# Weights of a later stage split into two parts ahead of time and kept in DRAM

## Chip, cores and metric

The kernel runs on one NeuronCore of one Trainium2 chip. The metric is device time in microseconds (us), the median of several executions.

## Reference

The computation is ten stages over one activation of 512 tokens by 1024 features, in fp32. The first block has two layers, each a mixer and a feed-forward; the second block has two layers of its own, each a mixer, a cross-attention to 256 memory tokens and a feed-forward. What matters here is the first block:

```
for l in range(2):                                   # first_block
    h = rmsnorm(x, norm_mix_g[l]);  proj = h @ w_in[l]          # "mixer": 1024 -> 4896 columns
    qa, ka, va, qd, kd, vd, beta, decay, z, gates = split(proj)
    y_attn = grid_attention(rope(rms(qa)), rope(rms(ka)), va) @ w_o_attn[l]
    o = bidir_gated_deltanet(conv(qd), conv(kd), conv(vd), sigmoid(beta), decay)
    y_dn = (rmsnorm(o) * silu(z)) @ w_o_dn[l]
    x = x + (sigmoid(g0) * y_attn + sigmoid(g1) * y_dn) @ w_out[l]
    h = rmsnorm(x, norm_ffn_g[l]);  u_gate, u_val = conv3(h @ w_up[l])   # "feed-forward"
    x = x + (silu(u_gate) * u_val) @ w_down[l]
```

## The kernel before

Activations lie transposed: eight tiles of 128 features by 512 tokens. The stages run in the order m0, f0, m1, f1 (first block), ev, xa0, g0, od, xa1, g1 (second block); `body` calls them one after the other. The framework builds each engine's instruction order from the order of the program and a simulated timeline, so instructions of later code can stand ahead of earlier code on an engine.

Every product of weights and activations is made of three TensorE passes: each fp32 value is split into a high part (rounded to the fast matmul format) and a low part (what is left), and `proj` (L487 to L495) adds high x high, high x low and low x high. Activations are split once. A weight group is 1024 rows by 256 columns (1 MiB). `fetch` (L463) loads it by one transfer on SP's queue (L465) into one of two buffers `wraw`. `wload` (L469) then cuts it into four pieces of 128 x 512 (two column halves, two row halves); for each, ScalarE casts the high part `whi` (L478) and GpSimd subtracts for the low part `wlo` (issued through the helper at L384). `whi` and `wlo` have four buffers each, that is one group. TensorE uses a piece for 12 matmuls, and a group for 48.

A mixer (`_mix`) uses 19 such groups of `w_in`: four for keys and queries of the delta rule (`qk_pair`), two for its values (`vproj`), two for z (`zproj`), one for attention's k and v (`qkv`), two for its queries (`queries`), and eight for the gates (`gate_logits`). Only the first four run alone. The others are generators that a class `Side` advances beside the long chains: `inside` (the chunks of the delta rule, which stores many small blocks to DRAM: `dn`, `scrN`, `scrT`), `solve` (a triangular solve on DVE, which begins with the loads of `N` from `scrN` and `scrT`, L1023 and L1024), `core` (attention) and `scan` (the states of the delta rule). After the scan come the branch products (`w_o_attn`, `w_o_dn`) and `w_out`.

A feed-forward (`ffn`) makes its 22 pairs of tiles in 11 steps `up_pair` (two groups each), and multiplies by `w_down` in three parts `down` through `out_proj` (four groups each): after 5, 9 and 11 pairs. The weights are laid out in DRAM by the host (`_pack_cols`) so that a group is one contiguous run of 8 KB in each partition; a piece is then four runs of 128 elements.

Of the kernel before, what the change touches and what calls it, by code (L numbers as in the profile page):

```python
# [44 lines left out]
def _pack_cols(w, kc, cg):  # L45

    w = np.asarray(w)
    L, K, N = w.shape
    g = N // cg
    a = w.reshape(L, kc, P, g, cg).transpose(0, 3, 2, 1, 4)  # L50
    return np.ascontiguousarray(a).reshape(L, g, P, kc * cg)


def _cols(v):
# [151 lines left out]
def host_arrays(inputs):  # L206
    g = lambda k: np.asarray(inputs[k])
    A = {}
    A["x"] = np.ascontiguousarray(g("x")[0].T).reshape(8, P, S)
    A["mem"] = _pack_cols(np.asarray(g("mem_2")).transpose(0, 2, 1), 8, NMEM)[0, 0]  # L210
    A["vec"] = _vec_layout(inputs)[1]
    A["cst"] = CST_ARR
    A["rope"] = np.ascontiguousarray(_rope_tables())
    A["rett"] = _ret_tables()
    A["hgm"] = _hg_masks()
    A["dsat"] = _dsa_tables()
    A["relb"] = np.concatenate([g("rel_bias_2"), np.ones((1, 8), np.float32)], axis=0)
    w = g("w_in")
    qa, ka, va = w[..., :512], w[..., 512:640], w[..., 640:768]
    qd, kd, vd = w[..., 768:1280], w[..., 1280:1792], w[..., 1792:2304]  # L220
    bd, z, gate = w[..., 2304:2336], w[..., 2336:2848], w[..., 2848:]

    by_head = lambda a: a.reshape(2, -1, 2, 2, 2, 64).transpose(0, 1, 2, 4, 3, 5).reshape(2, -1, 512)
    z = by_head(z)
    qa = qa.reshape(2, D, 4, P)[..., PERM_A].reshape(2, D, 512)
    ka = ka[..., PERM_A]
    A["win"] = _pack_cols(np.concatenate([kd, qd, vd, qa, ka, va, z, gate], axis=-1), 8, 256)
    A["wbd"] = _pack_cols(bd, 8, 32)
    A["woa"] = _pack_cols(g("w_o_attn"), 4, 128)
    A["wod"] = _pack_cols(by_head(g("w_o_dn").transpose(0, 2, 1)).transpose(0, 2, 1), 4, 128)  # L230
    A["wout"] = _pack_cols(g("w_out"), 8, 256)
    A["wup"] = _pack_cols(g("w_up"), 8, 256)
    for nm, key in (("wdn", "w_down"), ("fdn", "ffn_w_out_2")):
        w = g(key)
        A[nm] = np.concatenate([_pack_cols(w[:, :1024], 8, 256), _pack_cols(w[:, 1024:2048], 8, 256)], axis=1)
        A[nm + "c"] = _pack_cols(w[:, 2048:], 6, 256)
# [3 lines left out]
    A["evin"] = _pack_cols(np.concatenate(ev, axis=2).reshape(1, D, 4096), 8, 256)  # L240
    A["evout"] = _pack_cols(np.concatenate([eo[:, 1 - i, h] for i, h in EV_HEADS], axis=1), 8, 256)

    od = g("od_w_in_2").reshape(1, D, 3, 8, P).transpose(0, 1, 3, 2, 4).reshape(1, D, 3072)
    A["odin"] = _pack_cols(od, 8, 256)
    A["odout"] = _pack_cols(g("od_w_out_2"), 8, 256)
    A["xaq"] = _pack_cols(g("xa_w_q_2"), 8, 256)
    A["xakv"] = _pack_cols(g("xa_w_kv_2"), 8, 256)
    A["xao"] = _pack_cols(g("xa_w_o_2"), 8, 256)
    A["fup"] = _pack_cols(g("ffn_w_in_2"), 8, 256)
    return A  # L250


# [53 lines left out]
class Prog:  # L306
    def __init__(self, ctx, tc, A, out, first):
        self.ctx, self.tc, self.nc, self.A, self.out = ctx, tc, tc.nc, A, out
        nc = self.nc
        pool = lambda name, bufs=1, **kw: ctx.enter_context(tc.tile_pool(name=name, bufs=bufs, **kw))  # L310
        self.cp = pool("cp")
        self.xp = pool("xp")
        self.wr = pool("wr", 2)
        self.whl = pool("whl", 4)
        self.actp = pool("actp", 8)
        self.nrm = pool("nrm")
        self.psb_ = pool("psb", 2, space=PSUM)
        self.dr = pool("dr", 1, space=DRAM)
        self.ph = None
        self.mem = {}  # L320
# [139 lines left out]
        return ps  # L460


    def fetch(self, src, kc, cg):  # L463
        raw = self.wr.tile([P, kc, cg], F32, name="wraw", tag="wraw")
        self.nc.sync.dma_start(out=raw, in_=src.rearrange("p (k c) -> p k c", k=kc))  # L465
        return raw

    def wload(self, src, kc, cg, rows=False):


        nc = self.nc
        raw = self.first.pop(0) if self.first else self.fetch(src, kc, cg)
        step, width = (2, cg) if rows else (4, min(P, cg))

        def piece(k, o):
            part = raw[:, k:min(k + step, kc), o:o + width]
            hi, lo = (self.whl.tile(list(part.shape), F32R, name=n, tag=n) for n in ("whi", "wlo"))
            nc.scalar.copy(hi, part)  # L478
            self.tt(lo, part, hi.bitcast(F32), ALU.subtract, "gpsimd")
            return k, hi, lo  # L480

        return [[piece(k, o) for k in range(0, kc, step)] for o in range(0, cg, width)]

    def proj(self, ps, w, acts, n=S, behind=None):

# [48 lines left out]
    def out_proj(self, wsrc, acts, nxt, k0=0, scale=None, final=True, behind=None):  # L534
        nc = self.nc
        kc = len(acts)
        for g in range(4):
            ws = self.wload(wsrc[g][:, k0 * 256:(k0 + kc) * 256], kc, 256)
            for j in range(2):
                m = 2 * g + j  # L540
                ps = self.psb()
                self.proj(ps, ws[j], acts, behind=behind)
                if scale is None:
                    self.tt(self.x[m], ps, self.x[m], ALU.add)
                else:
                    nc.vector.scalar_tensor_tensor(self.x[m], ps, scale, self.x[m], ALU.mult, ALU.add)
                if final:
                    self.x_done(m, nxt)

    def x_done(self, m, nxt):  # L550
        nc = self.nc
# [10 lines left out]
    def ffn(self, l, second, nm, nxt):  # L562
# [3 lines left out]
        with self.phase("ffn") as fp, self.banks(2, 2):  # L566
# [48 lines left out]
            def up_pair(mp):  # L615
                wg = self.wload(wup[mp], 8, 256)
                wv = self.wload(wup[11 + mp], 8, 256)
                for j in range(2):
                    v = (up2 if second else up1)(2 * mp + j, wg[j], wv[j])
                    mid = self.gs("mid", 12, (P, 2, S), F32R)  # L620
                    self.split(mid, v)
                    mids[2 * mp + j] = mid

            def down(gi):
                ks = range(8 * gi, min(22, 8 * gi + 8))
                src = [wdn[gi * 4 + i] for i in range(4)] if gi < 2 else [wdnc[i] for i in range(4)]
                self.out_proj(src, [mids[k] for k in ks], nxt, final=gi == 2)

            for mp in range(5):
                up_pair(mp)  # L630
                if mp == 2 and l == 0 and second:
# [6 lines left out]
            down(1)  # L638
            for mp in range(9, 11):
                up_pair(mp)  # L640
            down(2)


# [4 lines left out]
    def _mix(self, l, nm, nxt, mp):  # L648
        nc, tc = self.nc, self.tc
        win = self.A["win"][l]  # L650
        col = lambda name, n=64: mp.tile([P, n], F32, name=name)
        blk64 = self.c("blk64")

# [52 lines left out]
        kq = []  # L706

        def qk_pair(g, first, a):
            ws = self.wload(win[g], 8, 256)
            for j in range(2):  # L710
                if a == 0:
                    kq.append(kv("kq", (first + j) // 2))
# [95 lines left out]

        def vproj():
            for g in range(4, 6):  # L810
                ws = self.wload(win[g], 8, 256)
                for j in range(2):
                    p = 2 * (g - 4) + j
                    c = th("cv", 2)
# [79 lines left out]
        def qkv():  # L894


            ws = self.wload(win[8], 8, 256)
# [18 lines left out]
        def queries(g):  # L916


            ws = self.wload(win[6 + g], 8, 256)
            qs = []  # L920
            for w in ws:
                qs.append(gained(w, f"qg{l}"))
# [66 lines left out]

        def zproj():  # L990
            for g in range(9, 11):
                ws = self.wload(win[g], 8, 256)
                for j in range(2):
                    if j == 0:
                        zz = kv("z", 0)
# [6 lines left out]

        def gate_logits(base, res, make):
            for g in range(4):
                ws = self.wload(win[base + g], 8, 256)
# [650 lines left out]
    def _cross(self, l, nm, nxt, xp):  # L1656
# [30 lines left out]
        for h in range(4):  # L1687
# [14 lines left out]
            ws = self.wload(wkv[4 + h], 8, 256, rows=True)  # L1702
            vt = [gs("vt", 4, (P, 2, M), F32R) for _ in range(2)]
            pv = [self.psb() for _ in range(2)]
            for t in range(2):
                tok = slice(t * P, (t + 1) * P)
                o = pv[t][:, :M]
                for k, hi, lo in ws[0]:
# [96 lines left out]
```

## Time and profile before

| | |
|---|---|
| median of 3 runs | 3369.54 us (3366.3 to 3373.71) |
| profiled execution: its time | 3364.51 us |
| its span, first to last instruction | 3362.7 us |
| mean granted TensorE clock | 0.986 of full |
| PE / DVE / ACT / POOL busy | 95% / 55% / 45% / 51% |
| f0 in the trace | about 480 to 885 us |
| m1 in the trace | about 885 to 1345 us |

PE is TensorE's matmuls, DVE is VectorE, ACT is ScalarE, POOL is GpSimd, SP is the engine whose queue issues nearly all transfers. Busy time of PE is modelled from its starts, so a PE that shows as fully busy is one that is never left waiting, not one at its peak. In a view of stretches, the number after a busy time is the count of instructions, PEclk is the granted clock as a share of full speed, and the DMA share is the mean busy share of the 16 DMA engines.

### The profile page before, as it was taken

Reading aid. Unit: us, or ns where it says so; the run is one execution under the profiler, and the core shown is the slowest. Engines: PE = TensorE matmul, PEld = TensorE weight load, DVE = VectorE, ACT = ScalarE, POOL = GpSimd, SP = SyncE. Lnnn points to the kernel's source line nnn. Section 1 sums busy time; section 2 is a strip of 40 time slices with the busy share of each in tenths; the row PEclk is TensorE's granted clock in tenths of the full one; section 3 lists DMA queues with packets and bytes.
Section 4 is the critical chain, followed back from the end, with each engine's and each line's share of the span. In section 5 each row is a group of like instructions: output and inputs, shape, how many; then the busy total and the mean of one; then the engine's idle time right before and its main releaser. Section 6 shows DMA issues by size and latency. Waiting matters only on the chain. (4 is left out here: it accounts for less than half of the span.)

```text
span 3362.7 us, 47054 instructions
## 1 busy us (share of the span) xinstructions
PE 3198.5 (95%) x17342; PEld 2643.8 (79%) x17342; DVE 1832.8 (55%) x3549; ACT 1499.9 (45%) x2804; POOL 1719.1 (51%) x1453
## 2 busy tenths in 40 slices
PE   8988799999998889999999998999999999999999
PEld 6767678888776677788887777878888888888887
DVE  7687556463678855555366675453223676453222
ACT  5646444343564643443353335543334455544332
POOL 4542375444554236544456556565556336555554
PEclk9999999999999999999999999999999999999999
DMA  4632532222355254322222113234223223222222
GB/s 155 179 94 67 136 118 99 97 92 94 125 162 136 69 124 129 126 90 99 100 102 88 63 47 129 91 124 132 90 99 110 73 69 126 95 91 93 99 100 88
DMA packets 142013, 353.03 MB, mean 105 GB/s; under 512 B 44079, under 2 KB 81327, under 8 KB 113112
## 3 DMA queue, kind: packets, MB, share of 16 engines
q1 hardware_dynamic: 140352, 346.53, 32.0%
q10 hardware_dynamic: 1432, 3.49, 0.4%
q8 instruction: 138, 2.26, 0.3%
q14 instruction: 91, 0.75, 0.1%
HBM read 316.34 MB, written 34.16 MB: 104 GB/s over the span
## 5 line engine op out<-in xcount | busy, mean ns | idle before, releaser
L384 POOL TENSOR_TENSOR wlo<-wraw,whi 128x512 fp32r<-128x512 f32 (+2 forms) x1044 | 1353.1, 1299 | 1420.8 <-ACT whi L478 1382.6
L478 ACT CAST whi<-wraw 128x512 fp32r<-128x512 f32 (+2 forms) x1044 | 633.4, 608 | 1141.0 <-PE psb L494 863.7
L491 PE MATMUL psb<-act,whi 128*128 128x512 f32 x1888 | 750.8, 398 | 25.4 <-ACT whi L478 12.6
L495 PE MATMUL psb<-act,wlo 128*128 128x512 f32 x1888 | 746.3, 396 | 0.6 <-POOL wlo L384 0.4
L494 PE MATMUL psb<-act,whi 128*128 128x512 f32 x1888 | 746.3, 395 | 0.6 <-DVE act L277 0.6
L491 PEld LDWEIGHTS psb<-act,whi 128*128 128x128 f32 x1888 | 359.0, 190 | 101.9 <-ACT whi L478 14.1
L495 PEld LDWEIGHTS psb<-act,wlo 128*128 128x128 f32 x1888 | 358.0, 190 | 76.5 <-POOL wlo L384 3.0
L494 PEld LDWEIGHTS psb<-act,whi 128*128 128x128 f32 x1888 | 358.6, 190 | 73.7 <-DVE act L277 2.0
L384 DVE TENSOR_TENSOR x<-psb,x 128x512 f32<-128x512 f32 x168 | 115.1, 689 | 380.3 <-PE psb L495 380.0
L491 PE MATMUL ps<-act,whi 128*128 128x512 f32 (+1 forms) x720 | 282.8, 393 | 3.4 <-ACT rB L303 3.4
L494 PE MATMUL ps<-act,whi 128*128 128x512 f32 (+1 forms) x720 | 282.2, 392 | 0.0
L495 PE MATMUL ps<-act,wlo 128*128 128x512 f32 (+1 forms) x720 | 281.9, 391 | 0.0
L491 PE MATMUL psb<-mid,whi 128*128 128x512 f32 x704 | 277.1, 394 | 1.0 <-DVE x L384 1.0
L495 PE MATMUL psb<-mid,wlo 128*128 128x512 f32 x704 | 276.3, 393 | 0.0
L494 PE MATMUL psb<-mid,whi 128*128 128x512 f32 x704 | 273.9, 389 | 0.0
L491 PEld LDWEIGHTS ps<-act,whi 128*128 128x128 f32 (+1 forms) x720 | 135.0, 188 | 34.3 <-ACT rB L303 4.9
L495 PEld LDWEIGHTS ps<-act,wlo 128*128 128x128 f32 (+1 forms) x720 | 135.0, 188 | 29.7
L494 PEld LDWEIGHTS ps<-act,whi 128*128 128x128 f32 (+1 forms) x720 | 135.0, 187 | 29.3
L495 PEld LDWEIGHTS psb<-mid,wlo 128*128 128x128 f32 x704 | 132.3, 188 | 30.5
L491 PEld LDWEIGHTS psb<-mid,whi 128*128 128x128 f32 x704 | 132.7, 188 | 29.2 <-DVE x L384 1.5
L494 PEld LDWEIGHTS psb<-mid,whi 128*128 128x128 f32 x704 | 132.2, 188 | 29.2
L384 DVE TENSOR_TENSOR cv<-ps,cv 128x512 f32<-128x512 f32 (+1 forms) x60 | 41.5, 692 | 188.7 <-PE ps L495 106.8
(431 smaller groups left out, 5441.9 us busy)
## 6 DMA issues: line engine op xcount, KB each, us to landing
wraw<-in_wup SPq DMA_DIRECT2D x44, 1024.0 KB, 4.8
wraw<-in_fup SPq DMA_DIRECT2D x44, 1024.0 KB, 4.8
wraw<-in_win SPq DMA_DIRECT2D x38, 1024.0 KB, 4.8
wraw<-in_wdn SPq DMA_DIRECT2D x16, 1024.0 KB, 4.8
wraw<-in_evin SPq DMA_DIRECT2D x16, 1024.0 KB, 4.8
wraw<-in_xakv SPq DMA_DIRECT2D x16, 1024.0 KB, 4.9
wraw<-in_fdn SPq DMA_DIRECT2D x16, 1024.0 KB, 4.9
wraw<-in_odin SPq DMA_DIRECT2D x12, 1024.0 KB, 4.8
```

Source lines behind the costliest of these rows:

```text
L384: getattr(self.nc, eng).tensor_tensor(out, a, b, op)
L478: nc.scalar.copy(hi, part)
L491: mm = nc.tensor.matmul(ps, hi[:, i], acts[k][:, 0, :n], start=k == 0, stop=False)
L494: nc.tensor.matmul(ps, hi[:, i], acts[k][:, 1, :n], start=False, stop=False)
L495: nc.tensor.matmul(ps, lo[:, i], acts[k][:, 0, :n], start=False, stop=k == kc - 1)
```

## The change

During f0, a generator `split_ahead` loads the 19 groups of `w_in` of layer 1, splits them and stores both parts to DRAM. It is advanced once after each `up_pair` and once after each group of the first two `down` parts (5 + 4 + 4 + 4 + 2 = 19 steps). A step loads two halves of 128 x 1024 (512 KB each), casts both on ACT, subtracts the first on DVE and the second on GpSimd, and issues the two stores (1 MiB each) of the step before. In m1, `wload_split` takes the place of `wload` for the 19 groups: eight transfers of 256 KB on SP's queue, straight into the four `whi` and four `wlo` buffers, with no cast and no subtraction. Also, the host lays out nearly all weights so that a piece is one contiguous run of 512 elements (`_pack_tiles`); the split of all other groups goes on as before, on such pieces. The stages m0 and all those from f1 on do the same work as before.

```diff
+def _pack_tiles(w, kc):
+    a = _pack_cols(w, kc, 256)
+    L, g = a.shape[:2]
+    return np.ascontiguousarray(a.reshape(L, g, P, kc, 2, P).transpose(0, 1, 2, 4, 3, 5)).reshape(L, g, P, kc * 256)
...
-    A["win"] = _pack_cols(np.concatenate([kd, qd, vd, qa, ka, va, z, gate], axis=-1), 8, 256)
+    A["win"] = _pack_tiles(np.concatenate([kd, qd, vd, qa, ka, va, z, gate], axis=-1), 8)
...
+    def fetch(self, src, kc, cg, k0=0, n=None):
+        n, w = n or kc, min(P, cg)
+        raw = self.wr.tile([P, cg // w, n, w], F32, name="wraw", tag="wraw")
+        self.nc.sync.dma_start(out=raw, in_=src.rearrange("p (j k c) -> p j k c", k=kc, c=w)[:, :, k0:k0 + n])
+        return raw
+    def parts(self, part):
+        nc = self.nc
+        hi, lo = (self.whl.tile(list(part.shape), F32R, name=n, tag=n) for n in ("whi", "wlo"))
+        nc.scalar.copy(hi, part)
+        self.tt(lo, part, hi.bitcast(F32), ALU.subtract, "gpsimd")
+        return hi, lo
+    def split_ahead(self, pool, name, groups):
+        nc = self.nc
+        late = []
+        for i, src in enumerate(groups):
+            dst = self.dr.tile([P, 2, 2, 1024], F32, name=f"{name}{i}")
+            self.ahead[name, i] = dst
+            for a in late:
+                nc.sync.dma_start(out=a[0], in_=a[1])
+            late = []
+            for j in range(2):
+                raw = pool.tile([P, 1024], F32, name="araw", tag="araw", bufs=2)
+                nc.sync.dma_start(out=raw, in_=src[:, j * 1024:j * 1024 + 1024])
+                t = pool.tile([P, 2, 1024], F32R, name="ahl", tag="ahl", bufs=4)
+                nc.scalar.copy(t[:, 0], raw)
+                self.tt(t[:, 1], raw, t[:, 0].bitcast(F32), ALU.subtract, ("vector", "gpsimd")[j])
+                late.append((dst[:, j], t.bitcast(F32)))
+            yield
+        for a in late:
+            nc.sync.dma_start(out=a[0], in_=a[1])
+    def wload_split(self, src):
+        def piece(j, k):
+            hi, lo = (self.whl.tile([P, 4, P], F32R, name=n, tag=n) for n in ("whi", "wlo"))
+            for i, t in enumerate((hi, lo)):
+                self.nc.sync.dma_start(out=t.bitcast(F32), in_=src[:, j, i, k * P:(k + 4) * P].rearrange("p (k c) -> p k c", c=P))
+            return k, hi, lo
+        return [[piece(j, k) for k in (0, 4)] for j in range(2)]
...
@@ out_proj, behind each group, and up_pair, at its end
+            if self.side:
+                self.side()
...
@@ ffn
+            later = iter(())
+            if not second and l == 0:
+                later = self.split_ahead(fp, "win", [self.A["win"][1][g] for g in range(19)])
+            self.side = lambda: next(later, None)
...
+            self.side = None
+            for _ in later:
+                pass
             down(2)
...
@@ _mix
+        wgroup = lambda g: self.wload_split(self.ahead["win", g]) if l else self.wload(win[g], 8, 256)
...
-            ws = self.wload(win[g], 8, 256)
+            ws = wgroup(g)
```

## Rows read from the trace of the kernel before

**Rows 1.** The page's busy times of the whole span

```profile
PE 3198.5 (95%) x17342; PEld 2643.8 (79%) x17342; DVE 1832.8 (55%) x3549; ACT 1499.9 (45%) x2804; POOL 1719.1 (51%) x1453
```

**Rows 2.** Busy times by stretch: start and end, length, PE, PEld, DVE, ACT, POOL

```profile
520.00:880.00 360.00, 358.96 (x1581) 295.78 (x1580) 189.22 (x220) 148.72 (x244) 184.56 (x144) 1.00 0.29 102
885.00:965.00 80.00, 80.00 (x417) 64.91 (x416) 63.73 (x122) 45.85 (x81) 34.57 (x28) 1.00 0.36 122
965.00:1050.00 85.00, 70.49 (x344) 58.80 (x343) 56.20 (x96) 49.78 (x99) 41.28 (x34) 0.90 0.71 183
1050.00:1110.00 60.00, 52.15 (x239) 40.99 (x237) 56.97 (x112) 26.75 (x51) 25.77 (x19) 0.97 0.27 83
1110.00:1190.00 80.00, 71.06 (x401) 57.99 (x401) 62.26 (x118) 51.49 (x109) 19.74 (x18) 1.00 0.23 61
1190.00:1285.00 95.00, 78.25 (x1344) 66.20 (x1343) 52.18 (x132) 43.03 (x103) 33.40 (x57) 0.96 0.55 128
```

**Rows 3.** Shorter stretches, same columns, then PEclk, DMA share, GB/s

```profile
970.00:980.00 10.00, 5.19 (x30) 4.33 (x29) 8.44 (x14) 6.46 (x14) 3.36 (x3) 0.76 0.60 186
982.00:1022.00 40.00, 40.00 (x211) 33.84 (x210) 28.37 (x39) 30.37 (x63) 27.36 (x23) 1.00 0.82 235
1000.00:1040.00 40.00, 36.25 (x176) 30.07 (x175) 21.70 (x41) 20.00 (x39) 21.75 (x18) 0.96 0.97 240
1030.00:1050.00 20.00, 11.28 (x39) 9.03 (x40) 12.85 (x25) 5.71 (x10) 5.13 (x4) 0.75 0.69 124
1110.00:1120.00 10.00, 7.28 (x48) 6.10 (x48) 9.06 (x16) 7.55 (x17) 0.00 (x0) 1.00 0.81 184
2044.00:2050.00 6.00, 6.00 (x27) 4.69 (x26) 3.45 (x4) 2.22 (x5) 6.00 (x5) 1.00 0.99 342
```

**Rows 4.** Costliest groups by shape in m1, 885 to 1345: POOL, then ACT

```profile
L384 POOL TENSOR_TENSOR wlo<-wraw,whi 128x512 fp32r<-128x512 f32 x99 | 131.9, 1337 | 189.2 <-ACT whi L478 181.5 <-PE psb L495 3.2 <-PE psb L494 1.9
...
L478 ACT CAST whi<-wraw 128x512 fp32r<-128x512 f32 x99 | 60.9, 618 | 78.7 <-PE psb L494 64.0 <-POOL wlo L384 4.6 <-PE ps L494 2.8
```

**Rows 5.** Who waited longest: PE, DVE in the stretch around the solve

```profile
PE ps L416 <- ACT cv L884: 6.0, 1, 6.0
...
DVE ps L384 <- DMA N<-scrT: 6.1, 1, 6.1
```

**Rows 6.** DVE in order of time: two sizes of the solve's products, twice each

```profile
1047.34 1.41 DVE L384 TENSOR_TENSOR ps<-N 128x168 f32<-128x168 f32 x1
...
1073.61 0.66 DVE L384 TENSOR_TENSOR ps<-N 128x476 f32<-128x476 f32 x1
...
1078.60 1.55 DVE L384 TENSOR_TENSOR ps<-N 128x476 f32<-128x476 f32 x1
...
1099.48 0.34 DVE L384 TENSOR_TENSOR ps<-N 128x168 f32<-128x168 f32 x1
```

**Rows 7.** Groups by shape in f0, 520 to 880: POOL, ACT, DVE

```profile
L384 POOL TENSOR_TENSOR wlo<-wraw,whi 128x512 fp32r<-128x512 f32 x126 | 169.2, 1343 | 168.7 <-ACT whi L478 167.6 <-PE psb L495 1.0
...
L478 ACT CAST whi<-wraw 128x512 fp32r<-128x512 f32 x125 | 77.3, 618 | 114.1 <-PE psb L494 83.9 <-POOL wlo L384 12.7 <-PE ps L494 8.9
...
L384 DVE TENSOR_TENSOR cv<-cv 128x512 f32<-128x512 f32 x22 | 28.4, 1290 | 0.4
...
L502 DVE TENSOR_TENSOR mid<-cv,mid 128x512 fp32r<-128x512 f32 x22 | 15.6, 708 | 7.9 <-ACT mid L500 7.5
```

**Rows 8.** Transfers: issues of 965 to 1050; then eight 256 KB loads, issue and landing

```profile
wraw<-in_win SPq DMA_DIRECT2D x5, 1024.0 KB, 8.7
...
N<-scrT SPq DMA_DIRECT2D x1, 1024.0 KB, 12.1
...
L1683 SPq DMA_DIRECT2D mact<-mact x8: 326/430/433, 2042.5 to 2045.7; - x8
...
DMA to landing us min/median/max: 4.2/4.8/7.3
```

**Rows 9.** Splits of contiguous pieces (`w_o_attn`), 1195 to 1290: min/median/max ns

```profile
L384 POOL TENSOR_TENSOR wlo<-wraw,whi x13: 1267/1287/1295, 1194.3 to 1288.2; 128x512 fp32r<-128x512 f32 x13
```

More of the change, by code (lines that the diff above doesn't have):

```diff
@@ L230, in host_arrays @@
     A["wod"] = _pack_cols(by_head(g("w_o_dn").transpose(0, 2, 1)).transpose(0, 2, 1), 4, 128)
-    A["wout"] = _pack_cols(g("w_out"), 8, 256)
-    A["wup"] = _pack_cols(g("w_up"), 8, 256)
+    A["wout"] = _pack_tiles(g("w_out"), 8)
+    A["wup"] = _pack_tiles(g("w_up"), 8)
     for nm, key in (("wdn", "w_down"), ("fdn", "ffn_w_out_2")):
         w = g(key)
-        A[nm] = np.concatenate([_pack_cols(w[:, :1024], 8, 256), _pack_cols(w[:, 1024:2048], 8, 256)], axis=1)
-        A[nm + "c"] = _pack_cols(w[:, 2048:], 6, 256)
+        A[nm] = np.concatenate([_pack_tiles(w[:, :1024], 8), _pack_tiles(w[:, 1024:2048], 8)], axis=1)
+        A[nm + "c"] = _pack_tiles(w[:, 2048:], 6)
     ev, eo = g("ev_w_in_2").reshape(1, D, 8, 4, P), g("ev_w_out_2").reshape(1, 2, 4, P, D)
     ev = [ev[:, :, 5]] + [ev[:, :, (slice(0, 4), [4, 6, 7])[i == 0], h] for i, h in EV_HEADS]
-    A["evin"] = _pack_cols(np.concatenate(ev, axis=2).reshape(1, D, 4096), 8, 256)
-    A["evout"] = _pack_cols(np.concatenate([eo[:, 1 - i, h] for i, h in EV_HEADS], axis=1), 8, 256)
+    A["evin"] = _pack_tiles(np.concatenate(ev, axis=2).reshape(1, D, 4096), 8)
+    A["evout"] = _pack_tiles(np.concatenate([eo[:, 1 - i, h] for i, h in EV_HEADS], axis=1), 8)
     od = g("od_w_in_2").reshape(1, D, 3, 8, P).transpose(0, 1, 3, 2, 4).reshape(1, D, 3072)
[L244 to L249, printed above, removed]
+    A["odin"] = _pack_tiles(od, 8)
+    A["odout"] = _pack_tiles(g("od_w_out_2"), 8)
+    A["xaq"] = _pack_tiles(g("xa_w_q_2"), 8)
+    w = g("xa_w_kv_2")
+    A["xakv"] = np.concatenate([_pack_tiles(w[..., :1024], 8), _pack_cols(w[..., 1024:], 8, 256)], axis=1)
+    A["xao"] = _pack_tiles(g("xa_w_o_2"), 8)
+    A["fup"] = _pack_tiles(g("ffn_w_in_2"), 8)
     return A
@@ L319, in __init__ @@
         self.ph = None
+        self.ahead, self.side = {}, None
         self.mem = {}
@@ L460, in spread @@
         return ps
-    def fetch(self, src, kc, cg):
-        raw = self.wr.tile([P, kc, cg], F32, name="wraw", tag="wraw")
-        self.nc.sync.dma_start(out=raw, in_=src.rearrange("p (k c) -> p k c", k=kc))
[L466 to L482, printed above, removed]
+    def fetch(self, src, kc, cg, k0=0, n=None):
[3 more added lines that the diff above has]
+        return raw
@@ new lines, in wload_split, with wload @@
+    def wload_split(self, src):
[5 more added lines that the diff above has]
+        return [[piece(j, k) for k in (0, 4)] for j in range(2)]
+    def wload(self, src, kc, cg=256, k0=0, n=None):
+        raw = self.first.pop(0) if self.first else self.fetch(src, kc, cg, k0, n)
+        n = raw.shape[2]
+        return [[(k, *self.parts(raw[:, j, k:min(k + 4, n)])) for k in range(0, n, 4)] for j in range(raw.shape[1])]
@@ L484, in proj, with wrows @@
+    def wrows(self, src, kc):
+        raw = self.wr.tile([P, kc, 256], F32, name="wraw", tag="wraw")
+        self.nc.sync.dma_start(out=raw, in_=src.rearrange("p (k c) -> p k c", k=kc))
+        return [(k, *self.parts(raw[:, k:k + 2])) for k in range(0, kc, 2)]
     def proj(self, ps, w, acts, n=S, behind=None):
@@ L537, in out_proj @@
         for g in range(4):
-            ws = self.wload(wsrc[g][:, k0 * 256:(k0 + kc) * 256], kc, 256)
+            ws = self.wload(wsrc[g], wsrc[g].shape[-1] // 256, k0=k0, n=kc)
             for j in range(2):
@@ L622, in up_pair @@
                     mids[2 * mp + j] = mid
+                self.side()
             def down(gi):
@@ L810, in vproj @@
             for g in range(4, 6):
-                ws = self.wload(win[g], 8, 256)
+                ws = wgroup(g)
                 for j in range(2):
@@ L894, in qkv @@
         def qkv():
-            ws = self.wload(win[8], 8, 256)
+            ws = wgroup(8)
             kr, sq = gained(ws[0], f"kg{l}")
@@ L916, in queries @@
         def queries(g):
-            ws = self.wload(win[6 + g], 8, 256)
+            ws = wgroup(6 + g)
             qs = []
@@ L991, in zproj @@
             for g in range(9, 11):
-                ws = self.wload(win[g], 8, 256)
+                ws = wgroup(g)
                 for j in range(2):
@@ L1004, in gate_logits @@
             for g in range(4):
-                ws = self.wload(win[base + g], 8, 256)
+                ws = wgroup(base + g)
                 for j in range(2):
@@ L1701, in _cross @@
                 self.split(kn[-1], x)
-            ws = self.wload(wkv[4 + h], 8, 256, rows=True)
+            ws = self.wrows(wkv[4 + h], 8)
             vt = [gs("vt", 4, (P, 2, M), F32R) for _ in range(2)]
@@ L1707, in _cross @@
                 o = pv[t][:, :M]
-                for k, hi, lo in ws[0]:
+                for k, hi, lo in ws:
                     for i in range(2):
```

## Prediction

> **What bounds the kernel now.** The page comes first: TensorE is busy for 95% of the span and no other engine for more than 55% [rows 1]. So splitting weights costs time only where a matmul waits, and the whole gain has to lie in the idle time of PE inside m1. The view of stretches gives that by stage [rows 2]. f0 is full: 358.96 of 360 us, which is 0.227 us for each of its 1581 matmuls, so a piece of 12 matmuls is worth 2.7 us and a group of 48 is worth 10.9 us. The start of m1, where the first groups are used, is full as well: 80.00 of 80. Behind it PE is idle for 85 - 70.49 = 14.5 us in 965 to 1050, 7.9 us in 1050 to 1110, 8.9 us in 1110 to 1190 and 16.8 us in 1190 to 1285, 48 us in all. The last of these is the scan, which uses `w_o_attn`, and the change leaves that as it is. So 31.3 us are within reach, about 0.9%.
>
> The rest is which wait ends last there. In m1 POOL spends 131.9 us on 99 low parts and ACT 60.9 us on 99 casts, and ACT stands another 64.0 us in front of a cast until PE lets a buffer go [rows 4]; ACT works in order, so what is behind such a cast waits as well. But PE itself hardly ever waits for a weight. It waits for the chains: once 6.0 us for an ACT square, and DVE stands 6.1 us in front of the solve until `N` has been read from DRAM [rows 5]. The short stretches show the places [rows 3]: 970 to 980, where the chunks of the delta rule begin (PE 5.19 of 10, granted clock 0.76, so part of it at 1.2 instead of 2.4 GHz after idle time); 982 to 1022, where PE is full; 1000 to 1040, where the DMA engines are full (share 0.97); and 1030 to 1050, the wait for `N` (PE 11.28 of 20, clock 0.75). From 1050 to 1110, the solve, DVE is the limit: 56.97 of 60 [rows 2].
>
> **The change part by part.**
>
> *What goes from m1.* 19 x 4 = 76 casts of 0.618 us, 47 us of ACT, and 76 subtractions of 1.337 us, 102 us of POOL [rows 4]. In the full stretches this is worth nothing. It counts in three places.
>
> (a) Start of the chunks, 970 to 980: 4.8 us of idle PE [rows 3]. Casts stand between the chain's steps on ACT, but the chain has other steps on DVE and POOL. Bounds 0 and -4.8; I take -2.
>
> (b) Solve. Its products read two operands from SBUF. The same size takes 0.66 or 1.55 us, 0.34 or 1.41 us, and the long ones lie beside a subtraction on POOL [rows 6]. The solve has 15 sizes, each twice; the differences within the pairs, read in the same view, add up to 6.4 us, and two other DVE operations there have 0.9 and 1.1 us of the same. Some of this lies beside POOL work that stays. DVE is the limit here, and PE's idle 7.9 us is the most that can come back. Bounds 0 and -7.9; I take -6, near the sum.
>
> (c) Attention, 1110 to 1190: PE idle 8.9 us, ACT 51.49 and DVE 62.26 of 80 [rows 2]. Some nine pieces are split here, 9 x 0.618 = 5.6 us of ACT. Bounds 0 and -8.9; I take -4.
>
> *What comes into m1.* (d) Each group is 2 MiB by transfer, not 1. In 965 to 1050 five groups are loaded [rows 8], so some 5.2 MB are added. The full rate is 102 / 0.29 = 350 GB/s in f0 [rows 2], and 342 / 0.99 = 345 GB/s for runs of 2 KB, the new size [rows 3]. That is 15 us of transfer in 85 us; in 1000 to 1040 it is 7 us, where 0.03 x 40 = 1.2 us are free [rows 3]. The read of `N` takes 12.1 us in that crowd already [rows 8], and DVE, ACT and PE stand behind it. Bounds 0 and +13; I take +4, two thirds of the 5.9 us, because loads issued behind `N` don't delay it.
>
> (e) A weight used to be two groups ahead, one raw and one split. Now it is one group ahead: a buffer is asked for when PE is done with it, and needed three pieces, 8.2 us, later. A load of 256 KB lands after 4.8 us (4.2 to 7.3) when eight are issued together [rows 8], so this is covered, except where SP is held. SP's work grows: 152 issues of 0.43 us [rows 8] are 65 us in 460, and each stands in order with the stores of the delta rule: a load that waits for PE holds the stores behind it, a store that waits for DVE holds the weights. Bounds 0 and +17 (the second rival); I take +1.
>
> *What comes into f0.* (f) 38 casts of 128 x 1024, at most twice 0.618 us each: 47 us of ACT on 148.72 of 360. 19 subtractions on POOL, at most twice 1.343: 51 us on 184.56. 19 on DVE, between twice 0.708 and twice 1.290 us, the fast and the slow two-operand row: 27 to 49 us on 189.22 [rows 2, 7]. The busiest stays under 68%. What hides them is that PE needs 8.2 us to come back to a buffer; one large operation ahead of a cast or a subtraction delays it by 2.7 us at most. PE's tiles have two buffers each and a tile takes 24 matmuls, 5.4 us, so an eviction held by 2.6 us is covered too. Transfers: a step adds 1 MiB of load and 2 MiB of store, 19 x 3.15 = 60 MB in 360 us, 166 GB/s on 102, a share of 0.76. In a step of `down` (one group, 10.9 us) it is 4.2 MB, 12 us at 350 GB/s: four such steps in a row fall 4 us behind. The slowest row for stores is 184 GB/s at a share of 0.81, that is 227 GB/s [rows 3]; then a step takes 15 us and four fall 17 us behind, more than the group (10.9 us) that weights are ahead. Bounds 0 and 2 x (17 - 10.9) = +12; I take 0, nearest to the rows of large runs.
>
> *Layout.* A contiguous piece was split already: `w_o_attn` takes 1287 ns on POOL [rows 9] against 1337 with mixed layouts [rows 4], and POOL is not the limit: 0.
>
> Sum: -2 - 6 - 4 + 4 + 1 + 0 = -7 us. The profiled execution took 3364.51 us, of which 1.8 lie outside the span, so 3357.5 by it. The runs shown have their median 5 us higher, at 3369.54; against that it is 3362.5, and I forecast 3362.
>
> **A rule against it.** Eight loads of 256 KB take the place of one of 1 MiB. The rows show eight such loads issued within 3.7 us and moving at 342 GB/s together [rows 3, 8], so 2 MiB need about 6 us of a group's 10.9. The Trainium skill, "DMA: Bandwidth & Descriptors", section "Rules for kernel authors", asks for at least 1 MiB in a transfer, and its section on the anatomy of a DMA gives each about 2 us fixed plus its bytes at 436 GB/s. By that page, an estimate, a load of 256 KB is 2.6 us and eight in a row 21 us, and m1 would wait on every group. The trace agrees with a fixed part, but shows that it overlaps.
>
> **The rivals.**
>
> *Nothing to be seen* (0.26). PE is full in most of m1, what is gained in the solve is lost before it to `N`: with (d) at +10 instead of +4 the sum is -1, so about 3368.
>
> *Weights come late* (0.19; slower). In 965 to 1050 a load of `w_in` takes 8.7 us to land in the middle [rows 8], more than the 8.2 us that a piece is ahead. Before, a raw group stood between; now PE waits. The place is 982 to 1022, where PE is full and 40 / 10.9 = 3.7 groups are used. At 12.1 us, as `N` has it, each group loses 3.9 us, 14 in all, and a store held on SP behind a waiting load makes `N` later by about one such loss more: some +17 us, 3362 + 17 = 3379. The point that decides is whether pieces land within 8.2 us there. Against it: they are four times smaller.
>
> *f0 pays* (0.09; slower). Stores run at 227 GB/s, or a cast waits for its raw half and ACT holds all others: +12, and 3374 or more.
>
> *Each load waits for the one before* (0.02; slower): 8 x 4.8 = 38 us in a group's 10.9, 27 us x 19 = 500 us slower. The eight loads speak against it [rows 3, 8]. It is what the page of the Trainium skill named above, "DMA: Bandwidth & Descriptors", would lead to if its fixed part could not overlap.
>
> *More comes back* (0.06): (a) to (c) in full without (d): -21.6, 3348.
>
> **How the numbers follow.** The forecast has 0.38 (own range 3352 to 3366). A measurement of this kernel can tell about 0.2%, 6.7 us, from no change. Faster: 0.38 + 0.06 = 0.44. Same: 0.26. Slower: 0.19 + 0.09 + 0.02 = 0.30. The range goes from 3345, just under the large gain, to 3386, where late weights and half of f0's loss come together.
>
> **What would show it.** Right: f0 as full as before, 0.227 us a matmul, with its DMA share near 0.76; no casts and low parts of `w_in` in m1; the pairs of the solve alike; DVE free earlier at 1110; PE's idle time in 1050 to 1190 down by about 10 us. Wrong: in m1 matmuls of L491 to L495 that wait for a transfer into `whi` or `wlo`; `N` landing more than 17 us after its issue; in f0 casts that wait for `araw`, or weights that land after more than 10 us. What would upset it altogether is another order of instructions in m1, since the framework orders by its own simulated time.

## The result, and the profile after

The changed kernel takes 3391.01 us (median of 4 runs, 3387.22 to 3396.37) against 3369.5 (3366.3 to 3373.71) for the kernel before: ratio 1.0072, 95% interval 1.0052 to 1.0092. It is slower, by 22 us; the prediction was 3362. The profiled execution took 3387.22 us, its span is 3385.4.

Where the 22 us arise is told by marks that both traces have. The first load of `w_out` in m0 is issued at 456.4 us in both. The first load of the third part of `w_down`, near the end of f0, comes at 822.8 us before and at 843.2 after: 20.4 later. The last load of `w_o_attn` at the end of m1 comes at 1283.9 and 1304.5: 20.6 later. So f0 loses 20.4 us, and m1 neither gains nor loses. The span is 22.7 us longer; the last 2.4 of these arise behind f1, where the work is the same and the traces of the kernels below also differ from before, by 0.3 to 6.7 us.

f0 in the view of stretches (columns as in [rows 2]; then granted clock, DMA share, GB/s), the same 360 us and the stretch in which all kernels below are compared:

```profile
520.00:880.00 360.00, 346.22 (x1490) 278.11 (x1489) 233.04 (x230) 167.45 (x259) 231.61 (x147) 1.00 0.70 253
500.00:850.00 350.00, 336.55 (x1451) 270.23 (x1450) 223.92 (x219) 162.95 (x248) 226.69 (x150) 1.00 0.73 261
```

PE made 1490 matmuls where it had made 1581 [rows 2]; at 0.227 us each the missing 91 are 20.7 us. No engine is near its limit over the stretch: DVE rose to 233 us of 360, POOL to 232. PE's weight loads show what was late (who waits for whom: us in total, times, longest):

```profile
PEld ps L543 <- POOL wlo L394: 11.8, 14, 2.0
PEld ps L539 <- ACT whi L484: 3.4, 5, 1.3
PEld ps L539 <- ACT rB L312: 3.0, 1, 3.0
PEld psb L543 <- POOL wlo L394: 2.4, 3, 1.1
PEld psb L539 <- ACT whi L484: 1.6, 1, 1.6
```

The weights of f0 itself are late, 17 times in their low part (14.2 us in all) and six times in their high part (5.0 us). The groups by shape, which answer to [rows 7]:

```profile
L394 POOL TENSOR_TENSOR wlo<-wraw,whi 128x512 fp32r<-128x512 f32 x121 | 179.0, 1489 | 108.4 <-ACT whi L484 98.1 <-PE psb L543 4.3 <-DMA araw<-in_win 4.0
L394 POOL TENSOR_TENSOR ahl<-araw,ahl 128x1024 fp32r<-128x1024 f32 x19 | 48.4, 2548 | 16.5 <-ACT ahl L502 16.5
...
L394 DVE TENSOR_TENSOR ahl<-araw,ahl 128x1024 fp32r<-128x1024 f32 x18 | 27.4, 1523 | 15.1 <-ACT ahl L502 15.1
L394 DVE TENSOR_TENSOR cv<-cv 128x512 f32<-128x512 f32 x22 | 23.9, 1087 | 0.4
L550 DVE TENSOR_TENSOR mid<-cv,mid 128x512 fp32r<-128x512 f32 x22 | 20.0, 910 | 4.5 <-ACT mid L548 3.8
```

POOL's new low parts take 2.55 us, as costed. But operations that the change doesn't touch changed too: f0's own low parts take 1489 ns after 1343 and `mid` on DVE 910 after 708, while the product `cv` is shorter, 1087 after 1290 [rows 7]. (The mean of all these products of DVE is longer; it stands below, with the runs.) One late weight, read in order of time on POOL, DVE, ACT and PE's weight loads (start, us; in brackets the idle time and what ended it):

```profile
643.52 2.81 POOL L394 TENSOR_TENSOR ahl<-araw,ahl 128x1024 fp32r<-128x1024 f32 x1 [1.23 <-ACT ahl L502]
...
643.32 0.75 DVE L643 SCALAR_TENSOR_TENSOR cv<-pad,vect,cv 128x512 f32<-128x512 f32 x1
644.10 2.78 DVE L394 TENSOR_TENSOR cv<-cv 128x512 f32<-128x512 f32 x1
...
646.91 0.62 ACT L548 CAST mid<-cv 128x512 fp32r<-128x512 f32 x1 [3.47 <-DVE cv L394]
647.44 1.66 ACT L484 CAST whi<-wraw 128x512 fp32r<-128x512 f32 x3
...
648.11 0.19 PEld L539 LDWEIGHTS psb<-mid,whi 128*128 128x128 f32 x1 [1.63 <-ACT whi L484]
```

A DVE product with both operands in SBUF, 0.68 us at its shortest, takes 2.78 us here: it starts beside POOL's subtraction and ends 0.55 us after POOL does (646.88 against 646.33, though spans on POOL are rough in a profile). ACT stands in order in front of its result, three casts of weights stand behind ACT's `mid`, and PE waits.

In m1, the stretches of [rows 2] (and, last, of 970 to 980 in [rows 3]), 20.4 us later:

```profile
905.40:985.40 80.00, 76.81 (x397) 61.17 (x397) 59.33 (x128) 31.10 (x55) 2.05 (x2) 1.00 0.60 184
985.40:1070.40 85.00, 74.03 (x358) 60.52 (x356) 50.57 (x92) 38.62 (x78) 16.07 (x15) 0.94 0.90 245
1070.40:1130.40 60.00, 55.00 (x257) 45.14 (x258) 53.13 (x123) 21.95 (x41) 7.29 (x5) 0.97 0.57 171
1130.40:1210.40 80.00, 71.89 (x400) 58.95 (x399) 56.11 (x116) 46.13 (x98) 7.41 (x9) 0.98 0.32 89
...
990.40:1000.40 10.00, 10.00 (x51) 8.35 (x50) 6.84 (x12) 3.06 (x5) 1.04 (x1) 1.00 0.52 164
```

POOL is nearly free (2.05 us where it had 34.57), and the hole at the start of the chunks is closed (10.00 of 10 where it was 5.19). But the first 80 us lose 20 matmuls, the DMA share rises from 0.71 to 0.90 in the second stretch, and `N` comes later. The solve's own pairs, as in [rows 6]:

```profile
1073.10 0.34 DVE L394 TENSOR_TENSOR ps<-N 128x168 f32<-128x168 f32 x1
...
1095.76 0.67 DVE L394 TENSOR_TENSOR ps<-N 128x476 f32<-128x476 f32 x1
...
1100.41 0.67 DVE L394 TENSOR_TENSOR ps<-N 128x476 f32<-128x476 f32 x1
...
1123.14 0.34 DVE L394 TENSOR_TENSOR ps<-N 128x168 f32<-128x168 f32 x1
```

All are short now, and the solve takes 54.0 us (from the clearing of part of `N` at 1071.1 to the copies behind it at 1125.1) where it took 65.1 (1040.4 to 1105.5). It begins 10.3 us late by its own stage: 1071.1 - 20.4 - 1040.4.

### The profile page after: what moved, and what is told of

Its sections match the earlier page's. It is cut to its first block, busy times and chain, and to the rows that moved or that the text cites. A ratio compares the mean times of both kernels' runs of the same rounds, so it can differ in the third digit from the quotient of the medians.

```text
span 3385.4 us, 47312 instructions
## 1 busy us (share of the span) xinstructions
PE 3212.6 (95%) x17342; PEld 2647.2 (78%) x17342; DVE 1867.7 (55%) x3568; ACT 1494.9 (44%) x2766; POOL 1684.1 (50%) x1396
## 5 line engine op out<-in xcount | busy, mean ns | idle before, releaser
L394 POOL TENSOR_TENSOR wlo<-wraw,whi 128x512 fp32r<-128x512 f32 (+2 forms) x968 | 1270.0, 1317 | 1209.5 <-ACT whi L484 1167.9
L484 ACT CAST whi<-wraw 128x512 fp32r<-128x512 f32 (+2 forms) x968 | 587.3, 609 | 1048.3 <-PE psb L542 802.7
L543 PEld LDWEIGHTS ps<-act,wlo 128*128 128x128 f32 (+1 forms) x720 | 135.2, 188 | 41.3 <-POOL wlo L394 11.8
```

The source lines that it names most:

```text
L394: getattr(self.nc, eng).tensor_tensor(out, a, b, op)
L543: nc.tensor.matmul(ps, lo[:, i], acts[k][:, 0, :n], start=False, stop=k == kc - 1)
```

## The experiments

All were compared with the kernel before on the same chip. "Matmuls" is PE's count in 500 to 850 us of each trace; missing ones are worth 0.227 us each. m0 ends within 4 us of the same time in all, so the column compares f0 to a few matmuls. What is done behind 850 us isn't in it: of e6, whose steps reach to 873 us, it misses a part. In e1, e3, e5, e9, e12, e13 and e15 m1 splits its own weights.

| run | edit | ratio [95%] | matmuls | missing, us |
|---|---|---|---|---|
| before | | 1 | 1541 | |
| after | the change | 1.0072 [1.0052, 1.0092] | 1451 | 20.4 |
| e1 | m1 splits its own | 1.0069 [1.0053, 1.0086] | 1451 | 20.4 |
| e2 | m1's part alone | 1.0009 [0.9998, 1.0021] | f0 as before | |
| e3 | transfers alone | 1.0055 [1.0037, 1.0072] | 1482 | 13.4 |
| e4 | all subtractions on DVE | 1.0043 [1.0025, 1.0062] | 1524 | 3.9 |
| e5 | no stores | 1.0129 [1.0114, 1.0144] | 1380 | 36.5 |
| e6 | steps held to their place | 1.0075 [1.0057, 1.0093] | 1463 | 17.7 |
| e7 | split a step late | 1.0054 [1.0038, 1.0071] | 1451 | 20.4 |
| e8 | 11 groups, held | 1.0047 [1.0030, 1.0064] | 1485 | 12.7 |
| e9 | POOL writes zeros | 1.0003 [0.9994, 1.0012] | 1517 | 5.4 |
| e10 | POOL in halves | 1.0071 [1.0055, 1.0086] | 1458 | 18.8 |
| e11 | 9 groups on DVE | 0.9990 [0.9981, 0.9999] | 1524 | 3.9 |
| e12 | zeros behind the cast | 1.0019 [1.0010, 1.0028] | 1524 | 3.9 |
| e13 | POOL copies | 1.0115 [1.0099, 1.0130] | 1368 | 39.3 |
| e14 | as e11, two bursts | 0.9992 [0.9983, 1.0001] | 1540 | 0.2 |
| e15 | twice the zeros of e12 | 1.0019 [1.0008, 1.0030] | 1529 | 2.7 |
| e16 | as e11, begun later | 0.9997 [0.9988, 1.0005] | 1529 | 2.7 |

### Which stage: e1, e2

Theory: the loss is f0's, and m1 comes out even. Rival: weights that come late in m1.

```diff
-        wgroup = lambda g: self.wload_split(self.ahead["win", g]) if l else self.wload(win[g], 8, 256)
+        wgroup = lambda g: self.wload(win[g], 8, 256)
```

> The 19 groups are split beside f0 and stored as in the change, but m1 loads and splits its own weights as before and reads none of the stored parts. If the whole loss is made in f0 and what m1 gains and loses cancels, the time is that of the change, 3385 to 3395 us, and the last load of w_o_attn comes about 20 us later than before. If m1's loads from the stored parts cost something of their own that the shorter solve only covers, it is lower.

```diff
-                later = self.split_ahead(fp, "win", [self.A["win"][1][g] for g in range(19)])
+                later = self.split_ahead(fp, "win", [self.A["win"][1][0]])
...
-        wgroup = lambda g: self.wload_split(self.ahead["win", g]) if l else self.wload(win[g], 8, 256)
+        wgroup = lambda g: self.wload_split(self.ahead["win", 0]) if l else self.wload(win[g], 8, 256)
```

> Beside f0 only the first group is split ahead, and all 19 groups of m1 read the parts of that one group, so m1's projections use wrong weights while their loads and products have the size of the change. By the trace of the change: f0 as before, the solve 11 us shorter, N some 10 us later: 3360 to 3375 us. If weights that come late in m1 were behind the loss (my second rival), it is near 3380.

e1 took 3389.0 us, the whole loss; e2 3368.54 against 3364.6. So the loss is f0's, and m1's part is worth nothing that can be seen: in e2 `N` is 8.0 us late by its own stage, the solve 9.4 us shorter, and PE waits 9.2 us for parts that haven't landed.

### Transfers or operations: e3, e4, e5

```diff
-                raw = pool.tile([P, 1024], F32, name="araw", tag="araw", bufs=2)
+                raw = pool.tile([P, 1024], F32, name="araw", tag="araw", bufs=6)
...
-                t = pool.tile([P, 2, 1024], F32R, name="ahl", tag="ahl", bufs=4)
-                nc.scalar.copy(t[:, 0], raw)
-                self.tt(t[:, 1], raw, t[:, 0].bitcast(F32), ALU.subtract, ("vector", "gpsimd")[j])
-                late.append((dst[:, j], t.bitcast(F32)))
+                late.append((dst[:, j], raw.unsqueeze(1).broadcast_to((P, 2, 1024))))
```

> The transfers beside f0 alone: the raw halves are loaded and each is stored twice, without casts and subtractions, so what is stored is not the parts, and m1 splits its own weights as before. If the queues on ACT and POOL make the loss, f0 is as before: 3364 to 3372 us. If the crowd of transfers makes it, 3382 to 3395 us, with f0 weights landing later than 7 us.

```diff
-                self.tt(t[:, 1], raw, t[:, 0].bitcast(F32), ALU.subtract, ("vector", "gpsimd")[j])
+                self.tt(t[:, 1], raw, t[:, 0].bitcast(F32), ALU.subtract, "vector")
```

> The change with both subtractions of a step on DVE, none on GpSimd. If the 2.55 us low parts on POOL, in front of the 1.5 us ones that the weights wait for, make the loss, it falls to about 5 to 10 us: 3374 to 3382 us. If the transfers or ACT make it, it stays: 3387 to 3395 us.

```diff
-                late.append((dst[:, j], t.bitcast(F32)))
+                late.append((dst[:, j, :, 0:16], t[:, :, 0:16].bitcast(F32)))
```

> The casts and subtractions beside f0 without the stores: of each part only 16 of 1024 columns are stored, so the stored parts are incomplete, and m1 splits its own weights as before. Two thirds of the added bytes are gone, and a step has no store to wait for. If the 2.55 us low parts on POOL make the loss, f0 still loses 10 to 20 us: 3376 to 3388 us. If the crowd of transfers makes it (or what it does to the raw halves that ACT waits for), f0 is nearly as before: 3364 to 3372 us.

e3 alone would have misled. With six raw buffers instead of two and nothing to wait for, its transfers ran denser than the change's (DMA share 0.98 in 550 to 600, where the change has 0.90), and PE waited 11.8 us for high parts, never for a low one: another loss than the one sought. e4 cleared f0: 3.9 us instead of 20.4, with the transfers as before. The rest of its 15.7 us lies in m1 (3.6) and behind f1, where the order of instructions came out differently; that part wasn't followed. e5 fell on neither side: with two thirds of the bytes gone f0 lost more, 36.5 us. The stores had slowed the steps down: the 19 steps load in 512 to 684 us now, one in 9 us, after 512 to 754, one in 13. So the loss doesn't need the bytes of the stores; that the operations make it, and cost more when more of them come in less time, is what e5 suggests and the runs below have to show. (A part of e5's size can be the granted clock, 0.97 over 500 to 850 us where the change has 1.00.)

### Their place and their waits: e6, e7, e8, e10

A theory from the trace was that the steps run ahead of their place (the last half is loaded at 754 us, though the program calls the last step behind the last pair, at about 820), another that ACT stands in order in front of halves that haven't landed (14.8 us), and POOL behind ACT's casts of them (16.5 us).

```diff
+                nc.vector.tensor_copy(raw[:, 0:1], self.pace)
                 nc.sync.dma_start(out=raw, in_=src[:, j * 1024:j * 1024 + 1024])
...
+                self.pace = self.x[2 * g + 1][:, 0:1]
                 self.side()
...
+                self.pace = mid[:, 0, 0:1].bitcast(F32)
                 self.side()
```

> The change, but a raw half is loaded only behind a copy of one element of the result of the step that calls it, so no step can run ahead of its place. If the loss comes from steps that run ahead (19 in 250 us instead of 360), f0 loses less than 6 us: 3365 to 3374 us. If it comes from the work as such, wherever it stands, it stays near 3385 us; the copies also hold SP's queue, which alone could cost some us.

```diff
+            for j, raw in enumerate(done):
...
                 nc.scalar.copy(t[:, 0], raw)
                 self.tt(t[:, 1], raw, t[:, 0].bitcast(F32), ALU.subtract, ("vector", "gpsimd")[j])
                 late.append((dst[:, j], t.bitcast(F32)))
+            for j in range(2 if src is not None else 0):
+                raw = pool.tile([P, 1024], F32, name="araw", tag="araw", bufs=3)
                 nc.sync.dma_start(out=raw, in_=src[:, j * 1024:j * 1024 + 1024])
+                raws.append(raw)
```

> The change, but a step casts and subtracts the halves that the step before loaded, with three raw buffers. If ACT and POOL lose time because they stand, in order, in front of a raw half that has not landed (14.8 us of ACT and 16.5 us of POOL in f0), these waits go and the loss falls to 10 us or less: 3368 to 3380 us. If the length of POOL's own operations makes it, it stays at 3385 to 3392 us.

```diff
-                later = self.split_ahead(fp, "win", [self.A["win"][1][g] for g in range(19)])
+                later = self.split_ahead(fp, "win", {g: self.A["win"][1][g] for g in (8, 6, 7, 11, 12, 13, 14, 15, 16, 17, 18)})
```

> Only the 11 groups that m1 uses behind the chunks are split ahead, one step behind each pair of tiles and with the loads held back as in the run before the last; the other eight are split in m1 as before. If f0's loss grows with the number and density of the steps, it falls below 5 us; the solve keeps its 11 us, and N is not late, because the crowd of loads before it is as before: 3355 to 3366 us. If the loss is one for each step, it is 11/19 of 20 us: 3370 us or more.

```diff
-                self.tt(t[:, 1], raw, t[:, 0].bitcast(F32), ALU.subtract, ("vector", "gpsimd")[j])
+                for c in range(1 + j):
+                    h = slice(c * 512, (c + 1) * 512 if j else 1024)
+                    self.tt(t[:, 1, h], raw[:, h], t[:, 0, h].bitcast(F32), ALU.subtract, ("vector", "gpsimd")[j])
```

> The change with POOL's subtraction in two operations of 512 columns. POOL's work is the same, but neither its queue nor DVE is held for more than 1.3 us at a time. If it is the length of one operation that counts (for DVE beside it or for the low parts behind it), the loss falls to about half: 3374 to 3382 us. If it is POOL's total work, it stays at 3385 to 3395 us.

Neither theory is borne out, nor is the length of one operation. Spread over the whole of f0 (loads from 545 to 873 us) the steps cost as much as run ahead: 1.0 us each in e6 (17 of them before 850) and 1.3 in e8 (ten), where the change has 20.4 / 19 = 1.1. (In e6 DVE itself stood 23.1 us in front of the copies that hold the loads, until POOL had done with the half, so part of e6's loss can be that; in e8 it didn't.) In e7 ACT's waits for raw halves fell to 3.4 us, and f0 lost the same 20.4. In e10 no operation of a step takes POOL over 1.8 us, and f0 lost 18.8. What all four keep is POOL's subtraction. In e8 `N` also came 13 us late by its own stage: the split loads of nearly three groups, 22 of 256 KB, had gone out in front of it.

### What of POOL's subtraction: e9, e12, e13, e15

The row at 644.10 suggests that POOL and DVE take turns at reading. An operation that only writes tells this apart from POOL's queue.

```diff
-                self.tt(t[:, 1], raw, t[:, 0].bitcast(F32), ALU.subtract, ("vector", "gpsimd")[j])
+                if j:
+                    for _ in range(2):
+                        nc.gpsimd.memset(t[:, 1].bitcast(F32), 0.0)
+                else:
+                    self.tt(t[:, 1], raw, t[:, 0].bitcast(F32), ALU.subtract, "vector")
```

> Beside f0 POOL writes zeros twice over the low part of the second half in place of the subtraction (the stored low parts are wrong, and m1 splits its own weights as before). POOL has work of about the same length in its queue, but that work reads nothing from SBUF. If the loss comes from POOL's queue (its long operation in front of the low parts that PE waits for), it stays: 3380 to 3390 us. If it comes from DVE's operations with two SBUF inputs, which stand still while POOL subtracts, and from ACT behind them in order, it goes: 3364 to 3372 us, with no DVE operation of f0 much over 2 us.

The other three differ from e9 in the middle lines: e12, e13 and e15 in this order.

```diff
+                    nc.gpsimd.memset(t.bitcast(F32), 0.0)
...
+                    for _ in range(2):
+                        nc.gpsimd.tensor_copy(t[:, 1].bitcast(F32), t[:, 0].bitcast(F32))
...
+                    for _ in range(2):
+                        nc.gpsimd.memset(t.bitcast(F32), 0.0)
```

> As the run with zeros, but POOL now writes them in one operation over both parts of the second half, behind ACT's cast (both stored parts of that half are wrong, and m1 splits its own weights as before). So POOL stands in order in front of the cast, as in the change, and then writes for about 1.9 us, but reads nothing from SBUF. If POOL's wait for the cast and what is queued behind it make the loss, it comes back: 3380 us or more. If the reading beside DVE makes it, it stays away: 3364 to 3370 us.

> The counterpart: POOL copies the high part into the low part's place, twice (the stored low parts of the second half are wrong, and m1 splits its own weights as before). It reads SBUF and waits for the cast, as the subtraction does. If what counts is that POOL reads SBUF beside DVE, most of the loss comes back, in the measure of the copies' length: 3374 to 3388 us at 2 us a pair. If reading two operands is needed, or the subtraction itself, it stays at 3364 to 3370 us.

> As the run that writes zeros behind the cast, with two such operations for each step, 3.6 us of POOL in place of the change's 2.55 us (both stored parts of the second half are wrong, and m1 splits its own weights as before). If POOL's time in its queue counts, f0 loses at least what it loses with the change: 3385 us or more. If only the time counts in which POOL and DVE's two-operand operations read SBUF, the loss stays at the 2 to 6 us of that run: 3366 to 3373 us.

e9 took 3366.63 us, and f0 lost 5.4: most of the loss was gone, but so was POOL's wait for the cast. e12 put that wait back. POOL's groups by shape in 500 to 800 us of e12, then of e15 and of e13:

```profile
L504 POOL MEMSET ahl<- 128x2048 f32 x19 | 34.4, 1811 | 10.5 <-ACT ahl L502 10.5
```

```profile
L505 POOL MEMSET ahl<- 128x2048 f32 x38 | 68.8, 1810 | 10.3 <-ACT ahl L502 9.0 <-PE ps L547 1.2
```

```profile
L505 POOL COPY ahl<-ahl 128x1024 f32<-128x1024 f32 x38 | 50.2, 1334 | 18.0 <-ACT ahl L502 17.9
```

In e15 POOL has 68.8 us of this work in its queue, more than the 48.4 of the change, waits for the cast as well, and beside it run the same transfers (DMA share 0.70 against 0.73): f0 lost 2.7 us. In e13, with 50.2 us of work that reads, it lost 39.3. So it is not POOL's time but POOL's reading. In e12, e13 and e15 alike the raw half comes free with ACT's cast instead of POOL's operation, so that doesn't explain why e13 differs from the other two; ACT's casts take 0.62 us in all of them and in the change.

DVE's own products say the same of every run. Worked out from the busy times by shape in 500 to 850 us, f0's products with both operands in SBUF (two `cv` steps of the convolution, the `cv` product and `mid`) take 1041 ns on average before and 1261 in the change. They take 1257, 1171, 1181, 1234 and 1162 in e6, e7, e8, e10 and e13, where POOL reads for the steps, but 1080, 1056, 1067 and 1078 in e4, e9, e12 and e15, where it doesn't. In e3, without operations, it is 996: its loss is of another kind. The mean tells the two sorts of run apart; it doesn't give the size of the loss.

One of these products also shows how long a single wait can be (minimum, median, longest ns in 490 to 860), the change first, e12 below:

```profile
L394 DVE TENSOR_TENSOR cv<-cv x21: 678/693/2777, 540.5 to 858.1; 128x512 f32<-128x512 f32 x21
```

```profile
L394 DVE TENSOR_TENSOR cv<-cv x22: 678/692/1783, 539.3 to 847.0; 128x512 f32<-128x512 f32 x22
```

Products of up to 1.8 us stay; the kernel before has them as well, where POOL reads for f0's own low parts alone. The longest is not what costs: in e10 none is over 1.9 us, and f0 lost 18.8. The size of e13 isn't settled: its PE waited for high parts (26.8 us), ACT stood 27.3 us in front of raw halves (14.8 in the change) and once 3.5 us in front of a `w_up` group that hadn't landed, SP held loads behind stores, and the granted clock fell to 0.96 over 500 to 850 us, so that reading alone need not make all 39.3.

### A version from it: e11, e14, e16

e11 and e14 advance the steps only behind the groups of the `down` parts, e16 only behind the pairs; the lines for that are left out here.

```diff
-                later = self.split_ahead(fp, "win", [self.A["win"][1][g] for g in range(19)])
+                later = self.split_ahead(fp, "win", {g: self.A["win"][1][g] for g in (7, 11, 12, 13, 14, 15, 16, 17, 18)})
...
-                self.tt(t[:, 1], raw, t[:, 0].bitcast(F32), ALU.subtract, ("vector", "gpsimd")[j])
+                self.tt(t[:, 1], raw, t[:, 0].bitcast(F32), ALU.subtract, "vector")
```

> Nine groups only (one of those used in the solve and the eight of the gates) are split ahead, both subtractions on DVE; the other ten are split in m1 as before, so that few of the added loads stand in front of N. By the run with all subtractions on DVE f0 loses 9/19 of 4 us, 2 us; N comes 0 to 4 us late, and the solve gains 4 to 8 us: 3358 to 3368 us, so a little faster than before or the same.

e14 and e16 also hold the first loads by a copy of one element, as e6 does: of the last `mid` before each of the first two `down` parts, and of the first pair's second `mid`.

> The nine groups of the run with the best time so far, on DVE alone, but in two bursts: the first four steps begin when the first w_down part does, the other five with the second, where DVE has little else to do. In that run f0 lost 4.0 us in its first 120 us; here it loses 0 to 1.5 us, and m1 gains the same 7 us: 3356 to 3362 us, faster than before by 0.1 to 0.3%.

> The nine groups on DVE once more, with the first load held until the second tile of the first pair is done, so that the first steps don't stand in front of f0's own first work. By the rows of the two other runs with nine groups f0 loses 1 to 3 us in place of 4.0, and m1 gains 4 to 7 us: 3357 to 3364 us, faster by 0.05 to 0.25%.

3362.09, 3362.6 and 3364.06 us against 3365 to 3366: at best 0.1% faster, and only e11's interval stays under 1, by 0.0001. e11 loses 4.0 us in f0 and gains 7.6 in m1 (solve 10.1 shorter, `N` 2.2 late); e14 loses 0.4, but its `N` is 4.3 late and m1 gains 3.8. So what e14 saved in f0 it gave back in m1, where `N` came later.

## Why the prediction was wrong

**The step that failed is (f), the price of f0.** I took 0, with +12 as the bound; it measured 20.4, beyond the bound. I added up each engine's own time (none over 68%) and allowed one operation of 2.7 us in front of a weight that had 8.2 us. Both counts were about right (POOL's part took 2.55 us on average, 2.95 at the longest), and neither was the limit. What I left out is that POOL's subtractions and DVE's operations with two SBUF operands take turns. Term (b) of the same prediction used just that for the solve, and [rows 7] held the warning: DVE products between 708 and 1290 ns. The Trainium skill, "SBUF — State Buffer", section "Who interferes with whom", states it as an exclusive lock between DVE instructions with two SBUF inputs and GpSimd instructions that read SBUF, not those that only write; e12, e13 and e15 agree, with 3.9, 39.3 and 2.7 us lost. The prediction's own sign for f0, casts that wait for `araw`, is there (14.8 us), but e7 took it down to 3.4 us and lost as much.

How near f0 was to that limit can be estimated from the shortest durations before. In 490 to 860 us of the trace of before:

```profile
L592 DVE SCALAR_TENSOR_TENSOR cv<-pad,vect,cv x44: 737/870/1266, 526.7 to 843.5; 128x512 f32<-128x512 f32 x44
L593 DVE SCALAR_TENSOR_TENSOR cv<-pad,vect,cv x44: 739/753/1840, 527.5 to 844.3; 128x512 f32<-128x512 f32 x44
L384 DVE TENSOR_TENSOR cv<-cv x22: 679/1188/1671, 536.3 to 845.1; 128x512 f32<-128x512 f32 x22
L502 DVE TENSOR_TENSOR mid<-cv,mid x22: 686/693/1021, 537.6 to 846.5; 128x512 fp32r<-128x512 f32 x22
...
L384 POOL TENSOR_TENSOR wlo<-wraw,whi x137: 733/1295/1797, 490.3 to 859.6; 128x512 fp32r<-128x512 f32 x131, 128x256 fp32r<-128x256 f32 x6
```

An `up_pair` has 4, 4, 2 and 2 of the DVE rows, 8.6 us, and 8 low parts, 10.4 us by their median: 19.0 of the 21.8 us that PE takes for its 96 matmuls. A step adds 2.4 us on POOL and 1.2 on DVE at their shortest, 3.6, where 2.8 are free. At one step in 13 us, 1.7 in a pair, 6.1 us come into 2.8; with all on DVE (e4) 4.1; with zeros (e12) 2.0, which fits; in e5 (2.4 steps in a pair) 8.6. By this estimate these four fall in the order that they have, but it doesn't give sizes: e4 would be 1.3 us a pair over, some 14 us in eleven pairs, and lost 3.9, no more than e12. It gives only 0.8 us a pair for one step in each, where e6 and e8 lost 1.0 and 1.3 a step; operations of a step that stand close together would do that, and in e6 DVE's wait in front of the copies, but neither was tried by itself. How the turns make weights late was followed for one weight only.

**What f0's loss consists of.** With POOL's subtractions replaced by writes, the transfers, casts, DVE's half and all waits together cost 3.9 us (e12), and e4 lost the same. So POOL's 19 subtractions cost the other 16.5, by difference. The transfers' part of (f) was sized rightly as small; their rate was not foreseen (share 0.73 over 500 to 850, up to 0.95, as the steps ran ahead), and e3 shows that still denser transfers cost 13.4 us by themselves, once six buffers let them run.

**m1.** The forecast was -7 with f0 at 0; it measured +0.2. (b): -6, measured 11.1 us off the solve, more than the idle time of PE that I had bounded it by. (d): +4, measured +10.3, near its upper bound of +13 (for which the prediction shows no working): `N` is asked for 4.2 us later and takes 18.1 us to land after 12.1 [rows 8]. (a): -2, and the hole of 4.8 us is closed. (e): +1, measured some 4.5 us in the first 80 us (20 matmuls), with 8.5 us of waits of PE in m1 for parts in transfer. Both marks named for the rival of late weights are there (the other is `N` landing more than 17 us after its issue), at a quarter of its price. (c): -4, measured about 0 (PE is busy for 71.89 of 80 us where it was 71.06). Layout: 0, and m0 ends at the same time to 0.1 us. So the rival "nothing to be seen" holds for m1 by itself, as e2 shows, and "f0 pays" for the whole, by another mechanism than I gave it. On the rule against it: the 2 us that the prediction takes from the Trainium skill's section on the anatomy of a DMA stand there for transfers that GpSimd issues, and these go out on SP's queue.

## What to carry to other kernels

Here POOL's reads and DVE's operations with two SBUF operands had a common budget, which the busy shares of the single engines (53% and 51% of f0 before) don't show: where POOL works on SBUF operands, add its time to that of DVE's two-operand operations, stage by stage, before work is put "beside" a full engine. When an experiment takes away what slowed the others down (here the stores), it can make a loss larger and hide its cause; an experiment that changes only what an operation reads, and keeps its time and its waits, comes closer to the cause.

## What the hardware showed that was not expected

A POOL operation that only writes, 1.81 us long and placed twice in each step, left DVE's products of f0 at 1078 ns on average (1041 before) and cost f0 2.7 us, while copies of 1.03 to 2.05 us in the same place went with 1162 ns and 39.3 us, not all of it by reading alone. Beside a 2.81 us subtraction on POOL a 0.68 us product on DVE took 2.78 us and ended 0.55 us after it.
